# Building the matrices of each state-space block one block ahead, and the last two g_b tiles by seven products, in a gated two-branch encoder layer

## The chip, the core and the metric

The kernel runs on one core of one Trainium2 chip. The metric is device time in microseconds for one execution. The core has a matrix engine (PE in the profile, with its weight loads shown apart as PEld), two engines for elementwise work (DVE and ACT), a third one that here issues transfers and clears buffers (POOL), and SP, which issues weight loads. Each engine works through its own program in order: an instruction that waits holds up everything behind it on its engine. Engines wait for each other through semaphores.

## What is computed

One layer of a two-branch encoder on x of 512 positions by 2048 channels, in float32. Cut to what matters here:

```python
h = rmsnorm(x, norm_g)
v, bg, cg, za, u, zb, ga, gb = split(h @ w_in)          # 2048 wide each; u and zb 1024
ya = bg * causal_depthwise_conv(cg * v, conv_w)
ya = (ya * silu(za)) @ w_out_a
yb = gelu(s5_scan(u, a_re, a_im, log_dt, b_re, b_im, c_re, c_im, d_skip))
yb = yb * sigmoid(yb @ w_glu + b_glu)
yb = (yb * silu(zb)) @ w_out_b
m = sigmoid(ga) * ya + sigmoid(gb) * yb
return rmsnorm(x + m @ w_o, final_g)
```

`s5_scan` is a diagonal complex recurrence of 64 states for each of 64 groups of 16 channels, with an input matrix B, an output matrix C and a skip term.

## The kernel before

**Precision and tiles.** Activations and weights are split into a high part in the matrix engine's fp32r format and a low part (what is left). A product of two such numbers is taken as high·high + high·low + low·high, so a direct product of one 128x1024 weight tile with 512 positions takes 24 matrix instructions of 128x512 (lines 859 to 861). Such a tile is called a half gemm here, since two of them (16 x 128 input channels) make one output tile of 128 channels. Each weight tile is loaded from DRAM as `w_raw`, cast by ACT into `w_hi` (line 689), and DVE then takes `w_lo = w_raw - w_hi` (line 706). Two such pairs are made ahead of the half gemm that is being issued.

In what follows, half gemms and their weight tiles are numbered in the order of the casts: 0 to 17 make u, 18 to 49 the 16 tiles of g_b, 50 to 65 the 8 tiles of z_b, 66 to 73 the GLU, 74 to 89 the product with w_out_b. In names of the program, tile 27 is `w_hi_1321`, 28 is `w_hi_1366`, 29 is `w_hi_1400`, 30 is `w_hi_1451` and 31 is `w_hi_1508`.

**Seven products.** Later stages (c_g, v, z_a, b_g, most of g_a) take two output tiles at a time as a 2x2 block product with seven multiplications in place of eight (`seven`, lines 1101 and 1106). Each product uses 8 instructions of 128x512 and 8 of 128x256. The sums of weights that this needs are made partly by accumulating transfers on POOL and partly on DVE (lines 593 and 597).

**The stage of the state-space branch.** While PE works through the g_b and z_b tiles (`gate` and the loop over m behind it), a background generator `ssm_blocks` issues the recurrence in four blocks of 16 groups. After each half gemm `step(RATE)` lets it issue about RATE = 5.5 us of elementwise work; a scheduler then orders the instructions of each engine. For each block the generator calls:

- `front`: products of C and B with powers of the transition. DVE makes `F` (tiles `ssm_f`, 128x640) and, through `ssm_t`, the input matrices; ACT copies them to `ssm_bb` (line 358) and `ssm_sl` (line 375).
- `table`: ACT copies 16 columns of a base table (line 439) and a magnitude tile `g` (line 442), and DVE doubles the table at levels 4, 5 and 6 (18 small operations).
- `pe1`: 16 matrix instructions with `ssm_sl` (line 387), which give each chunk's input, and 16 with `ssm_bb` and `F` (line 395).
- `post`: ACT copies the chunk inputs to `h` (line 408, 8 instructions), makes `mi` (line 419, 8 instructions) and `el` from `F` (line 428, 4 instructions).
- `scan`: DVE multiplies by the table, runs two hardware scans (line 483), multiplies again, and leaves the states `x` and `h`.
- `skip`: ACT makes the skip term (line 519).
- `pe2` and `result`: PE forms the output from `mi`, `el` and the states (lines 507 and 510), DVE adds the skip term.

Before the change, the order for block i is: front(i), pe2(i-1), table levels 4 and 5, result(i-1), pe1(i), table level 6, post(i), loads for i+1, scan(i), skip(i).

The gate of a g_b tile (line 997) is an ACT instruction that waits until both half gemms of the tile are finished; its result goes to DRAM. After the last block, `gelu` and the GLU follow. The product with w_out_b multiplies each of its 16 output tiles by 1 + gate and stores it to `tb_d`.

Of the kernel before, what the change touches and what calls it, by code (L numbers as in the profile page):

```python
# [1 line left out]

# [1 line left out]

# [8 lines left out]
AF = mybir.ActivationFunctionType  # L13
ALU = mybir.AluOpType
ADD, SUB, MUL = ALU.add, ALU.subtract, ALU.mult
# [4 lines left out]
KD = D // P  # L20
# [6 lines left out]
SLOT = 1024  # L27
EPS = 1e-6
MAGIC = 12582912.0
RATE = 5.5  # L30
PRATE = 1.6
R7 = 1.2
WARM = 9
NR4 = 37
NA = 0
NAB = 2
NB7 = 14
LEAST = 0.6
NP7 = 4
OSTEP = 4.2  # L40
KORD = (0, 4, 1, 5, 2, 6, 3, 7)
HL = L // 2
EARLY = 2


# [490 lines left out]

def ssm_blocks(blocks):

    blocks[0].loads()
    yield 1  # L540
    for i, k in enumerate(blocks):
        yield from k.front()
        if i:
            blocks[i - 1].pe2()
            yield
        yield from k.table((4, 5))
        if i:
            yield from blocks[i - 1].result()
        k.pe1()
        yield from k.table((6,))  # L550
        yield from k.post()
        if i + 1 < len(blocks):
            blocks[i + 1].loads_u()
            blocks[i + 1].loads()
        yield from k.scan()
        yield from k.skip()
    yield 1
    blocks[-1].pe2()
    yield 1
    yield from blocks[-1].result()  # L560
# [162 lines left out]
def hybrid_kernel(ctx: ExitStack, tc: tile.TileContext, xT, x, cvec, fg, wu, wu7, wabc,  # L723
                  wgz, wgb, wga, wo, par, bs_d, be_d, ce_d, out):
    nc = tc.nc
    tt, ts, stt = _ew(nc)
    act = nc.scalar
# [11 lines left out]
    def psum():  # L739
        t = psp.tile([P, L], F32, tag="ps", name="ps")  # L740
        return t
# [3 lines left out]
    def wide(name, shape=(P, 2, L)):  # L745
        t = r4b.tile(list(shape), F32, tag="r4", name=name)
        return t

    def tmp():
        if r4b:  # L750
            return wide("tmp")[:, 0]
        t = tp_ctx.tile([P, L], F32, tag="tmp", name="tmp")
        return t
# [9 lines left out]
    W = WStream(c, 2, 2)  # L763
# [4 lines left out]
    for j in range(NA):  # L768
        for h in range(2):
            W.add(wga[j, h])  # L770
    for j in range(KD):
        for h in range(2):
            W.add(wgb[j, h])
    for m in range(8):
# [4 lines left out]
    for j in range(KD):  # L779
        W.add(wgb[j, 2])  # L780
    for j in range(NA, NAB):
        for h in range(2):
            W.add(wga[j, h])
    for j in range(0, KD, 2):
        for i in range(4):
            W.add7(wabc[j, i, 0], wabc[j + 1, i, 0], wabc[j + 1, i, 1], wabc[j, i, 1])
        i = NAB + j - 2
        if NAB <= i < NB7:
            W.add7(wga[i, 0], wga[i + 1, 0], wga[i + 1, 1], wga[i, 1])
    for j in range(NB7, KD):  # L790
        for h in range(2):
            W.add(wga[j, h])
# [31 lines left out]
    tb_d = [drp.tile([P, 2, L], F32, name=f"tb{j}") for j in range(KD // 2)]  # L824
# [4 lines left out]
    bg = []  # L829
# [127 lines left out]
    ps = psum()  # L957
# [42 lines left out]

    for j in range(NA):
        gate(ga_d[j // 2][:, j % 2], RATE)
    for j in range(KD):
        gate(gb_d[j], RATE)
    zb = []
    for m in range(8):
        ps = hgemm(RATE)
        if m % 2 == 0:
            zt = c.r4.tile([P, 2, L], F32, tag="r4", name="zb")
        tz = tmp()  # L1010
# [6 lines left out]
    for m in range(8):  # L1017
        ps = psum()
        gemm(ps, yg)
        th, g = tmp(), tmp()  # L1020
# [14 lines left out]
    def combine(k, out, yag=False):  # L1035
        y, t = wide("h_sum"), wide("h_t", (P, 4, HL))
        for i in range(2):
# [5 lines left out]
        if yag:  # L1043
            yield
        y11, y12, y21, y22 = y[:, 0, :HL], y[:, 0, HL:], y[:, 1, :HL], y[:, 1, HL:]
        if not yag:
# [7 lines left out]
        for i in range(2):  # L1054
            p = c.r4.tile([P, 2, 2, HL], F32R, tag="r4", name="h_comb")
            act.copy(p[:, :, 0], t[:, 2 * i:2 * i + 2])
# [6 lines left out]
    gq = []  # L1063

    def fetch_gb():
        if len(gq) < KD:
            t = tmp()
            nc.gpsimd.dma_start(t, gb_d[len(gq)])
            gq.append(t)
# [5 lines left out]
    for j in range(KD):  # L1075
        ps = psum()
        gemm(ps, yb, steps=1.15)
        th = gq[j]
        stt(th, th, 1.0, ps, ADD, MUL)
        nc.gpsimd.dma_start(tb_d[j // 2][:, j % 2], th)  # L1080
        fetch_gb()
    for j in range(NA, NAB):
        gate(ga_d[j // 2][:, j % 2], 4.2)
# [4 lines left out]
    def blocks(ops, sums):  # L1088
        y = [[ops[k0 + k][:, :, l0:l0 + HL] for k in range(8)] for k0, l0 in ((0, 0), (8, 0), (8, HL))]
        return y + [[sums[k][i] for k in range(8)] for i in range(4)]  # L1090

    def product(ps, acts, first, last, steps=R7):
# [10 lines left out]
        for k in range(8):  # L1103
            a = acts[k]
            flat = len(a.shape) == 2
            nc.tensor.matmul(ps[:, HL:], lo[:, k], a[:, :HL] if flat else a[:, 0], start=False,  # L1106
                             stop=last and k == 7, skip_group_check=True)
        step(steps)

    def seven(name, acts, steps=R7):  # L1110

        Y11, Y21, Y22, T1, T2, T3, T4 = acts
        o = wide(name)
        e1, pb = wide("half"), psum()
        product(pb, Y11, True, False, steps)
        act.copy(e1[:, 0], pb)
        e2, pd = wide("half"), psum()
        product(pd, T1, True, False, steps)
        act.copy(e2[:, 1], pd)
        product(pb, T2, False, False, steps)  # L1120
        act.copy(e1[:, 1], pb)
        product(pd, Y22, False, True, steps)
        tt(e1[:, 1], pd, e1[:, 1], ADD)
        product(pb, T3, False, False, steps)
        tt(e2[:, 1], pb, e2[:, 1], ADD)
        pa = psum()
        product(pa, Y21, True, True, steps)
        tt(e1[:, 0], pa, e1[:, 0], ADD)
        for i, e in enumerate((e1, e2)):
            if i:  # L1130
                product(pb, T4, False, True, steps)
                act.copy(e2[:, 0], pb)
            v = e.rearrange("p b (h l) -> p b h l", h=2)
            ov = o[:, i].rearrange("p (b l) -> p b l", b=2)
            if i:
                stt(ov, v[:, :, 0], -1.0, v[:, :, 1], MUL, SUB)
            else:
                tt(ov, v[:, :, 0], v[:, :, 1], ADD)
        return o
# [24 lines left out]
    def gate2(o, j):  # L1164
        t = wide("tz")
        act.activation(t, o, AF.Tanh, scale=0.5)
        nc.gpsimd.dma_start(ga_d[j // 2], t)
        yield

    hb = blocks(hp, th7)  # L1170
    for j in range(0, KD, 2):
        cc = seven("cg", hb)
        v = seven("v", hb)
        bg.append(conv(cc, v, j))
        z = seven("za", hb)
        bg.append(silu(cc, z))
        b = seven("bg", hb)
        bg.append(out_a(cc, b, j))
        i = NAB + j - 2
        if NAB <= i < NB7:  # L1180
            bg.append(gate2(seven("ga", hb), i))
    while bg:
        step()

# [17 lines left out]
    for _ in range(3):  # L1202
        step()
    for j in range(NB7, KD):
        gate(ga_d[j // 2][:, j % 2], 4.3)
# [14 lines left out]
    for j in range(NP7):  # L1220
        if j % 2 == 0:
            fetch_m()
        ps = psum()
        gemm(ps, yap[:8], last=False, steps=3.3)
        gemm(ps, yap[8:], first=False, steps=3.3)
        g, t = (v[:, j % 2] for v in mq[j // 2])
# [9 lines left out]
    def two(name):  # L1236
        t = c.r4.tile([P, 2, 2, HL], F32R, tag="r4", name=name)
        return t
# [64 lines left out]
    for j in range(NP7, KD, 2):  # L1303
# [3 lines left out]
        o = seven("wa", yb7, 1.7 if end else R7)  # L1307
# [129 lines left out]
    for i in range(2):  # L1437
        f = c.r4.tile([P, 1024], F32, tag="r4", name="fg")
# [23 lines left out]
    for t in range(2):  # L1462
        for a, b in [(0, L)] if t == 0 else [(0, HL), (HL, L)]:
            ps = psum()[:, :b - a]
# [85 lines left out]
```

## Time and profile before

| what | value |
|---|---|
| median of 3 runs | 1661.87 us |
| lowest and highest run | 1661.63 and 1663.71 us |
| profiled execution, its own time | 1661.74 us |
| span of that execution in the trace | 1659.9 us |
| DVE busy | 1301.0 us, 78% |
| ACT busy | 797.6 us, 48% |
| POOL busy | 238.3 us, 14% |

The span runs from the first to the last recorded instruction of the profiled execution; 1.8 us of that execution lie outside it. An engine's busy time is a mean over stages with different limits. The trace gives start and duration of each instruction, what an engine waited for ahead of it, and the clock that PE was granted.

### The profile page before, as it was taken

The numbers are of one execution on the slowest core, as the hardware profiler recorded it, in microseconds if no ns is written. First come the engines' busy times: TensorE is split into PE (matmuls) and PEld (weight loads), VectorE is DVE, ScalarE is ACT, GpSimd is POOL, SyncE is SP. The second block draws the span as 40 slices with busy tenths as digits, with TensorE's granted clock in tenths as the row PEclk, the third lists the DMA queues.
The fourth block names the chain that finished last, engine by engine and source line by source line (L and its number), as shares of the span: only waits on it lengthen the run. The fifth ranks groups of instructions, "written<-read, shape, count | busy, mean of one in ns | idle before, by whom it ended". The sixth has DMA issues, their size and how long they took to land.

```text
span 1659.9 us, 22983 instructions
## 1 busy us (share of the span) xinstructions
PE 1636.8 (99%) x8700; PEld 1397.8 (84%) x8700; DVE 1301.0 (78%) x1751; ACT 797.6 (48%) x1097; POOL 238.3 (14%) x387
## 2 busy tenths in 40 slices
PE   9999998899999999999999999999999999999997
PEld 7887887788888888888888888888888888888886
DVE  8996887895865687877878777777878787888497
ACT  6433556355522355555445555544545544446334
POOL 0012343211021101010100101001010231122000
PEclk9999999999999999999999999999999999999999
DMA  8333563543364677777776777777776788997783
GB/s 312 117 102 87 146 177 115 133 140 77 134 215 134 165 186 205 186 205 206 206 203 178 207 192 201 201 202 215 184 210 180 290 272 239 268 320 252 234 329 102
DMA packets 93199, 320.62 MB, mean 193 GB/s; under 512 B 12672, under 2 KB 12928, under 8 KB 93088
## 3 DMA queue, kind: packets, MB, share of 16 engines
q1 hardware_dynamic: 58752, 204.65, 35.8%
q0 software_dynamic: 33616, 113.40, 29.7%
q8 instruction: 68, 1.11, 0.3%
q10 hardware_dynamic: 720, 1.10, 0.2%
q14 instruction: 43, 0.35, 0.1%
HBM read 287.51 MB, written 25.30 MB: 188 GB/s over the span
## 4 chain that ended last, share of the span: by engine, by line
PE 94%; ACT 2%; DVE 2%; issue 1%; DMA 0%; DVEq 0%; SPq 0%; ACTq 0%
PE ps L1101 34%; PE ps L1106 18%; PE ps L1324 10%; PE ps L859 9%; PE ps L860 9%; PE ps L861 9%; PE ps L944 2%; PE ps L942 2%; PE ps L943 2%; PE ps L387 1%; PE ps L395 1%; ACT w_hi L689 1%; DVE ssm_t L66 0%; DVE w_lo L706 0%; PE ps L510 0%
## 5 line engine op out<-in xcount | busy, mean ns | idle before, releaser
L689 ACT CAST w_hi<-w_raw 128x1024 fp32r<-128x1024 f32 (+2 forms) x459 | 478.7, 1045 | 662.0 <-PE ps L1101 281.1
L706 DVE TENSOR_TENSOR w_lo<-w_raw,w_hi 128x1024 fp32r<-128x1024 f32 (+2 forms) x459 | 556.5, 1214 | 193.1 <-ACT w_hi L689 189.6
L1101 PE MATMUL ps<-h_comb,w_hi 128*128 128x512 f32 x1408 | 352.5, 392 | 0.0
L1101 PEld LDWEIGHTS ps<-h_comb,w_hi 128*128 128x128 f32 x1408 | 253.2, 189 | 45.2
L861 PE MATMUL ps<-pair,w_lo 128*128 128x512 f32 x720 | 280.7, 390 | 3.3 <-DVE w_lo L706 3.3
L859 PE MATMUL ps<-pair,w_hi 128*128 128x512 f32 x720 | 280.8, 391 | 3.2 <-ACT w_hi L689 2.7
L860 PE MATMUL ps<-pair,w_hi 128*128 128x512 f32 x720 | 280.4, 390 | 0.4 <-DVE pair L66 0.4
L1101 PE MATMUL ps<-pair,w_hi 128*128 128x512 f32 x1056 | 264.4, 392 | 0.0
L1101 PEld LDWEIGHTS ps<-pair,w_hi 128*128 128x128 f32 x1056 | 190.1, 189 | 34.1
L1106 PEld LDWEIGHTS ps<-h_comb,w_lo 128*128 128x128 f32 x1408 | 192.1, 190 | 13.7
L1106 PE MATMUL ps<-h_comb,w_lo 128*128 128x256 f32 x1408 | 196.3, 282 | 0.0
L859 PEld LDWEIGHTS ps<-pair,w_hi 128*128 128x128 f32 x720 | 135.0, 188 | 33.3 <-ACT w_hi L689 3.3
L861 PEld LDWEIGHTS ps<-pair,w_lo 128*128 128x128 f32 x720 | 135.1, 188 | 32.6 <-DVE w_lo L706 4.4
L860 PEld LDWEIGHTS ps<-pair,w_hi 128*128 128x128 f32 x720 | 135.2, 188 | 28.9 <-DVE pair L66 1.0
L1106 PEld LDWEIGHTS ps<-pair,w_lo 128*128 128x128 f32 x1056 | 144.1, 190 | 10.3
L1106 PE MATMUL ps<-pair,w_lo 128*128 128x256 f32 x1056 | 147.2, 282 | 0.0
L66 DVE TENSOR_TENSOR half<-ps,half 128x512 f32<-128x512 f32 x132 | 90.6, 686 | 66.5 <-PE ps L1106 66.5
L673 POOL DMA_DIRECT2D w_raw<-in_wabc_dram x64 | 55.2, 862 | 555.4 <-DMA w_raw<-in_wabc_dram 379.0
L1324 PE MATMUL ps<-w_hi,pair 128*128 128x512 f32 x192 | 60.8, 389 | 0.0
L597 DVE TENSOR_TENSOR w_raw<-w_raw 128x1024 f32<-128x1024 f32 x44 | 53.9, 1225 | 1.5
L593 DVE TENSOR_TENSOR w_raw<-w_raw 128x1024 f32<-128x1024 f32 x44 | 53.9, 1224 | 1.5
L1324 PE MATMUL ps<-w_hi,m_half 128*128 128x512 f32 x160 | 50.8, 389 | 0.0
(218 smaller groups left out, 1750.9 us busy)
## 6 DMA issues: line engine op xcount, KB each, us to landing
w_raw<-in_wabc_dram SPq DMA_DIRECT2D x160, 512.0 KB, 4.3
w_raw<-in_wga_dram SPq DMA_DIRECT2D x76, 512.0 KB, 5.1
w_raw<-in_wabc_dram POOLq DMA_DIRECT2D x64, 512.0 KB, 6.3
w_raw<-in_wo_dram SPq DMA_DIRECT2D x52, 512.0 KB, 6.1
w_raw<-in_wgb_dram SPq DMA_DIRECT2D x48, 512.0 KB, 3.8
w_raw<-in_wgz_dram SPq DMA_DIRECT2D x24, 512.0 KB, 3.4
w_raw<-in_wga_dram POOLq DMA_DIRECT2D x24, 512.0 KB, 7.1
m_r<-m POOLq DMA_DIRECT2D x32, 256.0 KB, 5.7
```

Of the source, the lines that this page charges most:

```text
L66: return v.tensor_tensor(out=o, in0=a, in1=b, op=op)
L593: tt(out=b11["x"], in0=b11["x"], in1=s1["x"], op=ADD)
L597: tt(out=s1["x"], in0=b12["x"], in1=b11["x"], op=ADD)
L673: nc.gpsimd.dma_start(box["x"], src.rearrange("p a b -> p (a b)"), accum_op=ADD)
L689: nc.scalar.copy(hi[:, a:b], raw[:, a:b])
L706: nc.vector.tensor_tensor(out=lo[:, a:b], in0=raw[:, a:b], in1=hi.bitcast(F32)[:, a:b], op=SUB)
L859: nc.tensor.matmul(ps, hi[:, k], a[:, 0], start=first and k == 0, stop=False)
L860: nc.tensor.matmul(ps, hi[:, k], a[:, 1], start=False, stop=False)
L861: nc.tensor.matmul(ps, lo[:, k], a[:, 0], start=False, stop=last and k == 7)
L1101: nc.tensor.matmul(ps if flat else both, hi[:, k], a, start=first and k == 0, stop=False, skip_group_check=True)
L1106: nc.tensor.matmul(ps[:, HL:], lo[:, k], a[:, :HL] if flat else a[:, 0], start=False, stop=last and k == 7, skip_group_check=True)
L1324: nc.tensor.matmul(ps, l, r[:, k2, c0:c1], start=first and k2 == i == 0, stop=last and k2 == 1 and i == 2, skip_group_check=True)
```

## The change

The generator now makes the matrices of block i+1 between the chunk inputs of block i and its scan. `front(0)` stands ahead of the loop. Inside, the loads for the next block come first, then the table (levels 4 and 5, pe2 of the block in front, level 6, its result), `pe1(i)`, four steps of `front(i+1)`, the first two steps of `post(i)` (the copies to `h`), the rest of `front(i+1)`, the rest of `post(i)`, and the scan. RATE goes from 5.5 to 6.1.

The last two of the 16 g_b tiles leave the direct stage (`NGB = 14`). They are made in one call of `seven`, after the first round of c_g, v, z_a and b_g. Until then the two w_out_b tiles that belong to them go to `tb_d[7]` as they are; a new background step, `gate_b`, reads them back, takes tanh of the two g_b tiles on ACT, multiplies on DVE and writes them again. In the numbering above, z_b now follows at 46, the GLU at 62 and w_out_b at 70.

```diff
-RATE = 5.5
+RATE = 6.1
+NGB = 14
+GB7 = {0: 14}
...
 def ssm_blocks(blocks):
     blocks[0].loads()
     yield 1
+    yield from blocks[0].front()
     for i, k in enumerate(blocks):
-        yield from k.front()
+        last = i + 1 == len(blocks)
+        if not last:
+            blocks[i + 1].loads_u()
+            blocks[i + 1].loads()
+        yield from k.table((4, 5))
         if i:
             blocks[i - 1].pe2()
             yield
-        yield from k.table((4, 5))
+        if not last:
+            yield from k.table((6,))
         if i:
             yield from blocks[i - 1].result()
         k.pe1()
-        yield from k.table((6,))
-        yield from k.post()
-        if i + 1 < len(blocks):
-            blocks[i + 1].loads_u()
-            blocks[i + 1].loads()
+        f = k.table((6,)) if last else blocks[i + 1].front()
+        for _ in islice(f, 4):
+            yield
+        p = k.post()
+        for _ in islice(p, 2):
+            yield
+        yield from f
+        yield from p
         yield from k.scan()
         yield from k.skip()
...
-    for j in range(KD):
+    for j in range(NGB):
         for h in range(2):
             W.add(wgb[j, h])
...
             W.add7(wga[i, 0], wga[i + 1, 0], wga[i + 1, 1], wga[i, 1])
+        if j in GB7:
+            i = GB7[j]
+            W.add7(wgb[i, 0], wgb[i + 1, 0], wgb[i + 1, 1], wgb[i, 1])
...
-        th = gq[j]
-        stt(th, th, 1.0, ps, ADD, MUL)
+        if j < NGB:
+            th = gq[j]
+            stt(th, th, 1.0, ps, ADD, MUL)
+        else:
+            th = tmp()
+            act.copy(th, ps)
         nc.gpsimd.dma_start(tb_d[j // 2][:, j % 2], th)
...
+    def gate_b(o, j):
+        t, r = wide("tz"), wide("tb_w")
+        nc.gpsimd.dma_start(r, tb_d[j // 2])
+        act.activation(t, o, AF.Tanh, scale=0.5)
+        yield
+        stt(r, t, 1.0, r, ADD, MUL)
+        nc.gpsimd.dma_start(tb_d[j // 2], r)
+        yield
...
+        if j in GB7:
+            bg.append(gate_b(seven("gb", hb), GB7[j]))
```

In the changed kernel the lines shift: 859 to 861 become 876 to 878, 387 becomes 391, 395 becomes 399, 689 becomes 703, 706 becomes 720, 997 becomes 1014, 358 and 375 become 362 and 379, 408, 419 and 428 become 412, 423 and 432, 439 and 442 become 443 and 446.

**First place: PE, the first matrix instructions of block 0.** These are the last rows of a half gemm and the start of `pe1(0)`, before the change. `w_hi_1400` is tile 29.

```order
L859 MATMUL ps_1505<-pair_870,w_hi_1400 128x512
L860 MATMUL ps_1505<-pair_870,w_hi_1400 128x512
L861 MATMUL ps_1505<-pair_870,w_lo_1453 128x512
L387 MATMUL ps_1544<-ssm_ug_947,ssm_sl_1479 128x128
L387 MATMUL ps_1545<-ssm_ug_947,ssm_sl_1479 128x128
```

The same place in the changed kernel, where `w_hi_1336` is tile 27:

```order
L876 MATMUL ps_1422<-pair_870,w_hi_1336 128x512
L877 MATMUL ps_1422<-pair_870,w_hi_1336 128x512
L878 MATMUL ps_1422<-pair_870,w_lo_1368 128x512
L391 MATMUL ps_1544<-ssm_ug_947,ssm_sl_1415 128x128
L391 MATMUL ps_1545<-ssm_ug_947,ssm_sl_1415 128x128
```

`pe1(0)` has moved from behind half gemm 29 to behind half gemm 27.

**Second place: ACT, at the same point.** Before the change; line 997 is the gate, `tmp_1502` that of half gemms 26 and 27, `tmp_1673` that of 28 and 29.

```order
L689 CAST w_hi_1400<-w_raw_1319 128x1024
L997 ACTIVATE tmp_1394<-ps_1318 128x512
L997 ACTIVATE tmp_1502<-ps_1397 128x512
L689 CAST w_hi_1451<-w_raw_1364 128x1024
L689 CAST w_hi_1508<-w_raw_1398 128x1024
L358 COPY ssm_bb_1437<-ssm_ft_1428 64x8x16 x4
L375 COPY ssm_sl_1479<-ssm_t_1480 64x8x64 x2
L439 COPY ssm_rr_1490<-ssm_base_1244 128x8x16
L439 COPY ssm_ri_1491<-ssm_base_1244 128x8x16
L442 COPY ssm_g_1495<-ssm_keep_304 128x1024
L689 CAST w_hi_1587<-w_raw_1449 128x1024
L375 COPY ssm_sl_1479<-ssm_t_1480 64x8x64 x2
```

In the changed kernel `tmp_1585` is the gate of 26 and 27, `tmp_1697` that of 28 and 29, and `w_hi_1425`, `w_hi_1508` and `w_hi_1591` are tiles 29, 30 and 31.

```order
L1014 ACTIVATE tmp_1585<-ps_1422 128x512
L703 CAST w_hi_1425<-w_raw_1334 128x1024
L703 CAST w_hi_1508<-w_raw_1364 128x1024
L379 COPY ssm_sl_1415<-ssm_t_1416 64x8x64 x2
L362 COPY ssm_bb_1403<-ssm_ft_1394 64x8x16 x4
L703 CAST w_hi_1591<-w_raw_1423 128x1024
L379 COPY ssm_sl_1415<-ssm_t_1416 64x8x64 x2
L1014 ACTIVATE tmp_1697<-ps_1588 128x512
L443 COPY ssm_rr_1488<-ssm_base_1244 128x8x16
L443 COPY ssm_ri_1489<-ssm_base_1244 128x8x16
L446 COPY ssm_g_1493<-ssm_keep_304 128x1024
L703 CAST w_hi_1648<-w_raw_1506 128x1024
```

The cast of tile 29 now stands behind the gate of half gemms 26 and 27 instead of ahead of it, and the start of the table stands behind the gate of 28 and 29 instead of ahead of it.

**Third place: ACT, ahead of the scan of block 0.** Before the change; `tmp_1745` is the gate of half gemms 30 and 31, `w_hi_1679` and `w_hi_1713` are tiles 33 and 34.

```order
L408 COPY ssm_h_1622<-ps_1555 64x512
L428 COPY ssm_el_1637<-ssm_f_1429 64x512
L419 ACTIVATE ssm_mi_1627<-ps_1564,cvec_t_75 32x8x64 x2
L419 ACTIVATE ssm_mi_1627<-ps_1564,cvec_t_75 32x8x48 x2
L419 ACTIVATE ssm_mi_1627<-ps_1564,cvec_t_75 32x8x32 x2
L419 ACTIVATE ssm_mi_1627<-ps_1564,cvec_t_75 32x8x16 x2
L428 COPY ssm_el_1637<-ssm_f_1433 64x512
L428 COPY ssm_el_1637<-ssm_f_1429 64x512
L428 COPY ssm_el_1637<-ssm_f_1433 64x512
L689 CAST w_hi_1679<-w_raw_1506 128x1024
L689 CAST w_hi_1713<-w_raw_1585 128x1024
L997 ACTIVATE tmp_1745<-ps_1676 128x512
```

In the changed kernel `w_hi_1745` is tile 34, `tmp_1899` the gate of half gemms 32 and 33, and `ssm_sl_1676` belongs to block 1.

```order
L703 CAST w_hi_1745<-w_raw_1646 128x1024
L379 COPY ssm_sl_1676<-ssm_t_1677 64x8x64 x2
L1014 ACTIVATE tmp_1899<-ps_1778 128x512
L379 COPY ssm_sl_1676<-ssm_t_1677 64x8x64 x2
L423 ACTIVATE ssm_mi_1687<-ps_1564,cvec_t_75 32x8x64 x2
L423 ACTIVATE ssm_mi_1687<-ps_1564,cvec_t_75 32x8x48 x2
L423 ACTIVATE ssm_mi_1687<-ps_1564,cvec_t_75 32x8x32 x2
L423 ACTIVATE ssm_mi_1687<-ps_1564,cvec_t_75 32x8x16 x2
L432 COPY ssm_el_1731<-ssm_f_1395 64x512
L432 COPY ssm_el_1731<-ssm_f_1399 64x512
L432 COPY ssm_el_1731<-ssm_f_1395 64x512
L432 COPY ssm_el_1731<-ssm_f_1399 64x512
```

The copies to `mi` and `el` of block 0 stood ahead of the gate of half gemms 30 and 31; they now stand behind the gate of 32 and 33. The scan's second product takes a buffer that the third of these `el` copies (the last reader of `ssm_f_1395`) sets free.

More of the change, by code (lines that the diff above doesn't have):

```diff
@@ L1 @@
 from contextlib import ExitStack
+from itertools import islice
 import numpy as np
@@ L1002, in hybrid_kernel @@
         gate(ga_d[j // 2][:, j % 2], RATE)
-    for j in range(KD):
+    for j in range(NGB):
         gate(gb_d[j], RATE)
@@ L1065, in fetch_gb @@
     def fetch_gb():
-        if len(gq) < KD:
+        if len(gq) < NGB:
             t = tmp()
```

## The prediction

> **What bounds the kernel now.** I read the page first, then PE's waits, then the stretches of the stage in which the change works, then the chain and the timelines there.
>
> ```profile
> span 1659.9 us, 22983 instructions
> PE 1636.8 (99%) x8700; PEld 1397.8 (84%) x8700; DVE 1301.0 (78%) x1751; ACT 797.6 (48%) x1097; POOL 238.3 (14%) x387
> PE 94%; ACT 2%; DVE 2%; issue 1%; DMA 0%; DVEq 0%; SPq 0%; ACTq 0%
> PE ps L387 <- ACT ssm_sl L375: 6.3, 3, 3.0
> PE ps L861 <- DVE w_lo L706: 3.3, 3, 1.4
> PE ps L859 <- ACT w_hi L689: 2.7, 2, 1.6
> ```
>
> PE is busy 99% of the span and is 94% of the chain. The last three rows say for whom PE waited: total, times, longest. There is little idle time to win: 12.3 us in these rows, and they lie in the state-space stage.
>
> ```profile
> 162.00:184.00 22.00, 20.78 (x129) 17.94 (x130) 16.91 (x26) 15.72 (x27) 15.06 (x26) 0.92 0.69 164
> 250.00:272.00 22.00, 17.30 (x122) 13.40 (x120) 16.82 (x28) 12.52 (x25) 1.19 (x3) 1.00 0.30 99
> 316.00:338.00 22.00, 19.01 (x154) 16.01 (x153) 19.97 (x39) 13.68 (x29) 3.88 (x8) 0.92 0.35 104
> sum 352.00, PE 339.52 PEld 279.62 DVE 282.45 ACT 169.54 POOL 82.61; mean PE 21.22 PEld 17.48 DVE 17.65 ACT 10.60 POOL 5.16
> ```
>
> Each row is a stretch: busy time of PE, PEld, DVE, ACT, POOL, then the granted clock. The sum, over 96 to 448 us, leaves PE 12.5 us idle. In that stretch DVE is 80% busy, so PE runs there with a second engine close behind. PE is held in three places, and the clock mean of 0.92 in two of the stretches is 8% of 22 us, 1.76 us lost in each: the price of half speed for twice that, 3.5 us. So a wait here costs its own length and something over 1.7 us behind it.
>
> The Trainium skill, page "TensorE: Matmul & The Clock Gate", section "Why this matters for your kernels", wants no idle gap over about 3 us between bursts of matmuls, since the clock gate then goes back to half. By that rule, which speaks against this change, each long wait costs its length plus a slow window; without it the sum below would be some 6 us less. The two 0.92 rows agree, and go further: there a longest wait of 3.0 us was enough.
>
> **What the seven products save.** The group of direct instructions in the stage, then starts of pieces on the chain:
>
> ```profile
> L859 PE MATMUL ps<-pair,w_hi 128*128 128x512 f32 x400 | 156.4, 392 | 3.2 <-ACT w_hi L689 2.7 <-ACT pair L760 0.5
> 1020.31 1.84 PE ps L1101 x8
> ...
> 1023.10 1.84 PE ps L1101 x8
> ...
> 420.10 0.23 PE ps L860
> ```
>
> The busy time of one instruction (392 ns) is no price, since neighbours overlap: the chain shows a direct one starting every 0.23 us, and a product, eight instructions of each kind, every 1023.10 - 1020.31 = 2.79 us and seven of them 19.5. A half gemm has 24 instructions: 24 x 0.227 = 5.44 us. Two g_b tiles are four half gemms, 21.8 us. The change removes 21.8 and adds 19.5: **-2.2 us** of PE work. ACT and DVE have three more weight tiles to split, beside seven more products; in the later stages no PE wait is in the list above, so I cost these, the two output tiles by copy, and the second pass over `tb_d[7]` at 0. What covers them is the background work's slack. If that cover is gone, the price is one 1.05 us tanh, one 1.22 us product and two transfers, bounded by their landing times in these rows:
>
> ```profile
> L1152 ACT ACTIVATE tz<-za 128x1024 f32<-128x1024 f32 x8 | 8.4, 1054 | 0.0
> L76 DVE SCALAR_TENSOR_TENSOR za<-tz,za 128x1024 f32<-128x1024 f32 x8 | 9.8, 1220 | 0.0
> tb_r<-tb POOLq DMA_DIRECT2D x8, 512.0 KB, 6.1
> ```
>
> So 0 to +14.5 us (1.1 + 1.2 + 6.1 + 6.1); below nothing it can't go, as all of it is added. I take 0, as the similar steps on z_a show 0.0 idle ahead.
>
> **The first seam: block 0's matrices (+8.6).** Rows of ACT, then one of DVE, then the chain:
>
> ```profile
> 150.10 0.60 ACT L997 ACTIVATE tmp<-ps 128x512 f32<-128x512 f32 x1 [9.56 <-PE ps L861]
> 150.59 1.99 ACT L689 CAST w_hi<-w_raw 128x1024 fp32r<-128x1024 f32 x2
> 157.73 1.23 ACT L358 COPY ssm_bb<-ssm_ft 64x128 f32<-64x128 f32 x4 [5.15 <-DVE ssm_ft L66]
> 158.98 1.25 ACT L375 COPY ssm_sl<-ssm_t 64x512 f32<-64x512 f32 x2
> 160.26 0.30 ACT L439 COPY ssm_rr<-ssm_base 128x128 f32<-128x128 f32 x1
> 160.67 1.04 ACT L442 COPY ssm_g<-ssm_keep 128x1024 f32<-128x1024 f32 x1
> 162.56 1.25 ACT L375 COPY ssm_sl<-ssm_t 64x512 f32<-64x512 f32 x2
> 151.66 1.23 DVE L706 TENSOR_TENSOR w_lo<-w_raw,w_hi 128x1024 fp32r<-128x1024 f32 x1 [7.42 <-ACT w_hi L689]
> 163.22 3.49 PE ps L387 x31
> 169.40 0.43 PE ps L859
> ```
>
> The gate at 150.10 is that of half gemms 26 and 27; ACT stood behind it for 9.56 us, and the casts and everything of `front(0)` behind them on DVE start only then. The path from there to the last `ssm_sl` (163.8) is covered by half gemms 28 and 29, which run to 161, so PE idles 2.3 us, then does `pe1(0)` at half clock (163.22 to 169.40, 6.2 us) and goes on.
>
> In the changed order `pe1(0)` stands right behind half gemm 27, and the cast of tile 29 has gone behind that same gate. DVE's second half of `front(0)` still begins at 151.66, with the subtraction for tile 29 in the place of tile 30's, and the path holds as many casts and subtractions as before. It loses the three copies of the table (160.26 to 161.6, 1.35 us), and the four to `bb` (1.23) now stand behind the first pair of `sl` instead of ahead: 163.8 - 2.6 = **161.1** for the last `sl`. PE has finished 27 at 150.1 and has nothing else in order: idle 11.0 us. `pe1(0)` takes 6.0, mostly at half clock, and half gemms 28 and 29 end at 161.1 + 6.0 + 10.9 = 178.0. The same work was done at 169.40 before: **+8.6**.
>
> **The second seam: table, `el` and scan of block 0 (+19.4).**
>
> ```profile
> 160.88 0.28 DVE L66 TENSOR_TENSOR ssm_rr<-ssm_rr,ssm_keep 128x128 f32<-128x128 f32 x1
> 167.71 0.68 DVE L66 TENSOR_TENSOR ssm_ri<-ssm_ri,ssm_t 128x512 f32<-128x512 f32 x1
> 170.20 3.75 ACT L419 ACTIVATE ssm_mi<-ps,cvec_t 32x512 f32<-32x512 f32 x8
> 173.96 1.88 ACT L428 COPY ssm_el<-ssm_f 64x512 f32<-64x512 f32 x3
> 179.23 1.22 DVE L66 TENSOR_TENSOR ssm_t<-ssm_h,ssm_ri 128x1024 f32<-128x1024 f32 x1
> 195.42 1.23 DVE L706 TENSOR_TENSOR w_lo<-w_raw,w_hi 128x1024 fp32r<-128x1024 f32 x1
> 196.56 2.46 DVE L66 TENSOR_TENSOR ssm_h<-ssm_h,ssm_t 64x1024 f32<-64x1024 f32 x2
> 212.02 2.19 PE ps L387 x31
> 216.11 0.43 PE ps L859
> ```
>
> The table now starts behind the gate of 28 and 29, so at 178.5 instead of 160.3; the table (18 operations between the first two rows, 7.5 us with another one of 0.6 among them) and the first four of `front(1)` hold the low parts of tiles 32 and 33: I count 2.5 us of PE idle. Half gemm 33 ends at 178.0 + 4 x 5.44 + 2.5 = 202.3. Behind its gate ACT does two `sl` copies (1.2), the eight of `mi` (3.75) and three of `el` (1.9), to 210.3 with its handovers; then the buffer for the second scan product is free. From that product to the subtraction that stands behind the scan were 195.42 - 179.23 = 16.2 us, so tile 35's low part is ready at 210.3 + 16.2 + 1.2 = 227.7, and the states at 230.2. PE finishes half gemm 34 at 207.7, does `pe1(1)` (216.11 - 212.02 = 4.1), four instructions of `pe2(0)` and two of half gemm 35 until 214.7 at the latest, and then stands before tile 35's low part: **13.0 us idle**, 1.4 more at the states, and a slow window. Half gemm 36 starts at 238.6 and 37 at 244.1. Before, the same work was done at 216.11: a lag of 28.0, **19.4** more than at the first seam.
>
> **The blocks behind (+32.5), and the end.**
>
> ```profile
> 276.14 0.43 PE ps L860
> 337.23 0.43 PE ps L859
> ```
>
> Block 1 repeats the pattern: its table start stands behind the gate of half gemms 36 and 37 (250), tile 39's low part behind that table (261.2, where PE is ready at 254.9: 5.5 idle, 1.3 slow), `mi` and `el` behind 39's gate, the scan from 281.9 to 300.6, and tile 42's low part behind it. Half gemm 43 starts at 307.5 and 46 at 323.8. Before, `pe1(2)` was over at 276.14 and half gemm 46 began 14 instructions (3.2 us) later, at 279.3: lag 44.5, +16.5. Block 2 again: table behind the gate of 45 (324.5), 5.9 us idle and 1.3 slow for tile 47, scan from 351.8, states at 370.5 with PE idle for 11.2, half gemm 54 at 399.1 against 338.6 (337.23 and six instructions more): lag 60.5, +16.0. Behind the last block nothing is moved; of before's own waits there some 1 us of 1.4 goes.
>
> The full sum is 8.6 + 19.4 + 32.5 - 1.0 - 2.2 = +57.3, or 1661.74 + 57.3 = 1719 us. What I trust least in it is the wait for `el`: where the buffers come free earlier than I read, seams two to four cost only the tables' gates and a scan that partly fits beside two half gemms. The nearest measured bound for a scan that PE waits for is the old stretch from 250 to 272 with 4.7 us idle; with 8 for each (4.7, the slow window of 1.7, and about 1.5 for the table) the sum is 8.6 + 3 x 8 - 3.2 = +29.4, or 1691 us. I lean to the full walk, as its waits stand in the program's order, and go a quarter of the way to the other end: **1712 us**. The profiled execution (1661.74) is within 0.2 us of the median of the runs, 1661.87, so the sum is made against both alike.
>
> **Rivals.**
>
> (a) It does what it says: matrices ready early, so the 6.3 us for `ssm_sl` go, with the two slow windows (3.5 us), and the seven products save 2.2: 1661.7 - 12.0 = 1650 us. For it: that wait is PE's longest, and blocks 1 to 3 do get their matrices a block earlier. Against it: block 0's do not, and the scan's late end replaces them. Chance 0.08.
>
> (b) Only the first seam is lost and the rest is caught up, because DVE has 20% of slack: 8.6 - 2.2, less up to 4 us for `ssm_sl` in blocks 2 and 3: +2.4 to +6.4, or 1664 to 1668 us, slower than before though little. It decides if tables and `el` of blocks 1 to 3 turn out to be on time. Against it: DVE can't use slack while it stands behind ACT, and ACT stands behind gates of half gemms just done. Chance 0.10; about half of that is within 0.2%.
>
> (c) The later stage, not the scan, decides: the second pass over `tb_d[7]` holds a buffer and PE waits for it, up to 14.5 us on top of the lighter walk (1691): 1706. Chance 0.06; it lies inside the range.
>
> (d) The walk as it stands, with a lighter and a full end, 1691 to 1719: chance 0.76.
>
> **How the numbers follow.** The range has to hold 0.8: it takes (c) and (d), 0.82 together, with room on both sides. Below 1691 I allow 17 us, as the 8 us for each of three seams may be 2.3, the smallest wait that the old order shows at such a place; above 1719 a further 16, the 14.5 us of (c) and one slow window. That is **1674 to 1735 us**. Left out are (a) and (b), 0.18. About 0.2%, 3.3 us, is what a measurement of this kernel can tell from no change. Faster by more than that: (a), 0.08. Within it: the low half of (b), 0.05. Slower: the rest, 0.87.
>
> **What would show each step.** In the profile of the changed kernel: PE idle about 11 us just behind 150, released by `ssm_sl`; `pe1(0)` starting near 161 where it started at 163.2; the table's copies behind the gate near 178; the first scan's second product near 210, with the third `el` copy as its releaser; waits of PE for `w_lo` of 5 to 13 us in the g_b stage, and more 0.9 clocks; seven products in the place of four half gemms with no wait by them. If PE stays busy for 96% of the stretch from 96 to 448 us, I am wrong. If the wait near 150 is there and the later ones are not, it is (b); then my error is the scan's start, not the order.

## The result, and the profile after

The changed kernel takes **1726.26 us** (median of 4 runs, 1725.56 to 1726.78) where the kernel before took 1661.84 us in the same session: 1.0385 times as long, 95% interval 1.0367 to 1.0403, or some 64 us. The profiled execution has a span of 1724.4 us, 64.5 more than before.

The page of the changed kernel: the span, busy time of the engines, the granted clock in 40 slices, and the chain by engine.

```profile
span 1724.4 us, 23012 instructions
PE 1649.0 (96%) x8716; PEld 1407.5 (82%) x8716; DVE 1310.4 (76%) x1760; ACT 805.1 (47%) x1105; POOL 238.9 (14%) x387
PEclk9998988889999999999999999999999999999999
PE 88%; DVE 6%; ACT 3%; issue 2%; DMA 0%; POOL 0%; SPq 0%; DVEq 0%; ACTq 0%; POOLq 0%
```

PE is idle for 1724.4 - 1649.0 = 75.4 us, against 1659.9 - 1636.8 = 23.1 before: 52.3 us more. It is also busy for 12.2 us more, though the seven products take work away: that is work at a lower clock. Together these are the 64.5. Both lie early: below 9 tenths the clock is only in slices 4 and 6 to 9, counted from 0, so between 129 and 388 us.

The same stretch of the state-space stage, 96 to 448 us, in one row: length, busy time of PE, PEld, DVE, ACT, POOL with instructions, then the granted clock, the DMA share and GB/s.

```profile
96.00:448.00 352.00, 288.10 (x1546) 236.84 (x1546) 241.79 (x415) 136.37 (x231) 81.43 (x148) 0.91 0.41 106
```

PE idles for 63.9 us there (12.5 before), which holds nearly all of the 52.3. DVE and ACT are less busy too, 242 and 136 us where they were 282 and 170. So no engine became the bound; each waits for another. The top rows of three lists of the changed kernel say for whom, between 140 and 460 us: engine, line, waited for, total, times, longest.

```profile
PE ps L878 <- DVE w_lo L720: 33.0, 7, 12.0
PE ps L514 <- DVE ssm_h L70: 10.9, 1, 10.9
PE ps L391 <- ACT ssm_sl L379: 10.9, 1, 10.9
PE ps L511 <- issue: 5.6, 3, 2.9
```
```profile
DVE ssm_rr L70 <- ACT ssm_rr L443: 47.9, 3, 17.8
DVE w_lo L720 <- ACT w_hi L703: 33.0, 8, 12.5
DVE ssm_t L70 <- ACT ssm_el L432: 14.0, 2, 7.0
```
```profile
ACT tmp L1014 <- PE ps L878: 74.1, 7, 16.7
...
ACT w_hi L703 <- DMA w_raw<-in_wgb_dram: 15.6, 6, 4.9
...
ACT w_hi L703 <- DMA w_raw<-in_wgz_dram: 4.8, 3, 3.7
```

Read together they close a ring. PE waits 33.0 us for low parts that DVE makes; DVE waits 47.9 us, in three pieces, for the start of a table that ACT copies; ACT waits 74.1 us, in seven pieces, at the gate (line 1014) until PE has finished a half gemm. The last two ACT rows are weight tiles that were not there in time, 20.4 us; no such row stood in ACT's list before. The gates' wait did stand there:

```profile
ACT tmp L997 <- PE ps L861: 51.9, 6, 10.3
```

So what is new is less this wait than what stands behind it: DVE's list before had no row for the table or for `el`.

One turn of the ring, from the timelines of ACT, DVE and PE (start, duration, engine, instruction, idle time before it and its releaser):

```profile
178.18 0.60 ACT L1014 ACTIVATE tmp<-ps 128x512 f32<-128x512 f32 x1 [16.68 <-PE ps L878]
178.80 0.30 ACT L443 COPY ssm_rr<-ssm_base 128x128 f32<-128x128 f32 x1
...
201.14 1.05 ACT L703 CAST w_hi<-w_raw 128x1024 fp32r<-128x1024 f32 x1 [3.47 <-DMA w_raw<-in_wgb_dram]
...
204.76 0.60 ACT L1014 ACTIVATE tmp<-ps 128x512 f32<-128x512 f32 x1
...
207.50 3.75 ACT L423 ACTIVATE ssm_mi<-ps,cvec_t 32x512 f32<-32x512 f32 x8
211.27 2.52 ACT L432 COPY ssm_el<-ssm_f 64x512 f32<-64x512 f32 x4
```
```profile
179.13 0.29 DVE L70 TENSOR_TENSOR ssm_rr<-ssm_rr,ssm_keep 128x128 f32<-128x128 f32 x1 [17.78 <-ACT ssm_rr L443]
...
213.18 1.23 DVE L70 TENSOR_TENSOR ssm_t<-ssm_h,ssm_ri 128x1024 f32<-128x1024 f32 x1 [6.99 <-ACT ssm_el L432]
...
229.38 1.23 DVE L720 TENSOR_TENSOR w_lo<-w_raw,w_hi 128x1024 fp32r<-128x1024 f32 x1
```
```profile
160.91 4.21 PE L391 MATMUL ps<-ssm_ug,ssm_sl 64*128 64x128 f32 x32 [10.89 <-ACT ssm_sl L379]
...
230.66 0.79 PE L878 MATMUL ps<-pair,w_lo 128*128 128x512 f32 x1 [12.00 <-DVE w_lo L720]
```

PE started 10.89 us late at 160.91; so the gate came at 178.18; so the table, which needs nothing of PE, came at 178.80 and DVE stood 17.78 us for it. The gate of half gemms 32 and 33, the next but one, came at 204.76, with `mi` and `el` behind it; DVE stood 6.99 us for a buffer that the copies to `el` still read, did the scan, and only then the low part at 229.38, for which PE stood 12.00 us. That delays the gates behind it, and block 1 begins the same way.

The cast at 201.14 is the one late weight tile that lies on this path. The chain shows that it was issued late and was not slow: the load starts right behind the copies to `bb` and takes 3.42 us, where the median of such loads is 3.7.

```profile
197.38 0.30 ACT ssm_bb L362
...
197.70 3.42 DMA w_raw<-in_wgb_dram
```

### The profile page after: what moved, and what is told of

It is laid out like the page before. It is cut to its first block, busy times and chain, and to the rows that moved or that the text cites. A ratio compares the mean times of both kernels' runs of the same rounds, so it can differ in the third digit from the quotient of the medians.

```text
span 1724.4 us, 23012 instructions
## 1 busy us (share of the span) xinstructions
PE 1649.0 (96%) x8716; PEld 1407.5 (82%) x8716; DVE 1310.4 (76%) x1760; ACT 805.1 (47%) x1105; POOL 238.9 (14%) x387
## 4 chain that ended last, share of the span: by engine, by line
PE 88%; DVE 6%; ACT 3%; issue 2%; DMA 0%; POOL 0%; SPq 0%; DVEq 0%; ACTq 0%; POOLq 0%
PE ps L1122 34%; PE ps L1127 17%; PE ps L1356 9%; PE ps L878 8%; PE ps L876 8%; PE ps L877 8%; DVE ssm_t L70 2%; PE ps L961 1%; PE ps L960 1%; PE ps L959 1%; DVE ssm_h L70 1%; DVE ssm_h L487 1%; DVE w_lo L720 1%; ACT ssm_mi L423 0%; ACT ssm_sl L379 0%
## 5 line engine op out<-in xcount | busy, mean ns | idle before, releaser
L1122 PE MATMUL ps<-h_comb,w_hi 128*128 128x512 f32 x1440 | 360.6, 392 | 0.0
L878 PE MATMUL ps<-pair,w_lo 128*128 128x512 f32 x688 | 272.4, 396 | 33.7 <-DVE w_lo L720 33.7
L1122 PEld LDWEIGHTS ps<-h_comb,w_hi 128*128 128x128 f32 x1440 | 259.0, 189 | 46.3
L876 PE MATMUL ps<-pair,w_hi 128*128 128x512 f32 x688 | 271.8, 396 | 3.9 <-ACT w_hi L703 3.2
L877 PE MATMUL ps<-pair,w_hi 128*128 128x512 f32 x688 | 271.2, 394 | 0.2 <-DVE pair L70 0.2
L1122 PE MATMUL ps<-pair,w_hi 128*128 128x512 f32 x1080 | 270.4, 392 | 0.0
L1127 PEld LDWEIGHTS ps<-h_comb,w_lo 128*128 128x128 f32 x1440 | 196.5, 190 | 14.0
L1127 PE MATMUL ps<-h_comb,w_lo 128*128 128x256 f32 x1440 | 200.8, 282 | 0.0
L1127 PEld LDWEIGHTS ps<-pair,w_lo 128*128 128x128 f32 x1080 | 147.3, 190 | 10.5
L687 POOL DMA_DIRECT2D w_raw<-in_wabc_dram x64 | 55.3, 864 | 538.9 <-DMA w_raw<-in_wabc_dram 372.2
```

The costliest lines, as they stand in the source:

```text
L687: nc.gpsimd.dma_start(box["x"], src.rearrange("p a b -> p (a b)"), accum_op=ADD)
L876: nc.tensor.matmul(ps, hi[:, k], a[:, 0], start=first and k == 0, stop=False)
L877: nc.tensor.matmul(ps, hi[:, k], a[:, 1], start=False, stop=False)
L878: nc.tensor.matmul(ps, lo[:, k], a[:, 0], start=False, stop=last and k == 7)
L1122: nc.tensor.matmul(ps if flat else both, hi[:, k], a, start=first and k == 0, stop=False, skip_group_check=True)
```

## The experiments

Ratios are to the kernel before, run in the same session, with 95% intervals; a ratio is turned into microseconds by 1662 us. The difference of two ratios is uncertain by about 0.002, some 3.5 us.

| kernel | RATE | blocks | ratio | us |
|---|---|---|---|---|
| e2, before with RATE alone | 6.1 | old | 1.0045 [1.0032, 1.0059] | +7.5 |
| e1, seven products alone | 5.5 | old | 1.0055 [1.0041, 1.0068] | +9.1 |
| e7, both | 6.1 | old | 1.0037 [1.0023, 1.0051] | +6.1 |
| the change | 6.1 | new | 1.0385 [1.0367, 1.0403] | +64.0 |
| e3, the change | 5.5 | new | 1.0380 [1.0366, 1.0394] | +63.2 |
| e4, loads late | 6.1 | new | 1.0380 [1.0366, 1.0395] | +63.2 |
| e5, product in `sl` | 6.1 | new | 1.0382 [1.0368, 1.0396] | +63.5 |
| e6, e5 and post first | 6.1 | new | 1.0333 [1.0318, 1.0347] | +55.3 |
| e9, no gate wait | 6.1 | new | 1.0101 [1.0085, 1.0118] | +16.8 |
| e10, e7 with no gate wait | 6.1 | old | 0.9954 [0.9937, 0.9971] | -7.6 |
| e11, e6 with no gate wait | 6.1 | new | 1.0025 [1.0014, 1.0036] | +4.2 |
| e8, e7 with a rest | 6.3 | old | 1.0013 [1.0004, 1.0022] | +2.2 |
| e12, e7 with a gate moved | 6.1 | old | 0.9999 [0.9989, 1.0010] | -0.2 |

### The parts of the change: e1, e2, e7, e3

**e1** keeps the old blocks and RATE, and makes the last two g_b tiles by seven products.

```diff
 RATE = 5.5
+NGB = 14
+GB7 = {0: 14}
...
```

> The generator and RATE of before, with only the two g_b tiles by seven products. By my theory (the seven products save 2.2 us and everything beside them is hidden) 1659.6 us, 1658 to 1661, with the waits of the state-space stage as before. Rival (the second pass over tb_d[7], the three further weight tiles or the longer POOL queue make PE wait): 1662 to 1676, with a wait of PE near the first rounds of seven products.

**e2** is the kernel before with the new RATE and nothing else.

```diff
-RATE = 5.5
+RATE = 6.1
```

> The kernel before with RATE 6.1 and nothing else. In the program's order pe1 of block 0 then stands behind half gemm 27 as in the change, but the table, mi and el of block 0 stay ahead of the gates. By my theory only the first seam is lost: PE idle about 11 to 12 us near 150 and about 1671 us (1667 to 1676). Rival (the first wait too comes from the early matrices and their loads): no wait there beyond 3 us and about 1662 us.

**e7** is e1 with the new RATE: the whole change but for the order of the blocks.

```diff
 GB7 = {0: 14}
-RATE = 5.5
+RATE = 6.1
```

> The change without its generator: the blocks' order of before, RATE 6.1, the two g_b tiles by seven products. If the 12.3 us wait for the gelu's tiles in e1 is the cover of four half gemms that left the stage, and RATE 6.1 makes up for it, the wait is gone here and the time is that of e2 less 2.2: 1668.6 us (1667 to 1671), and the new order of the blocks alone costs 57 us of the change. Rival (the seven products cost some 9 us wherever they stand): 1680 us.

PE's longest wait between 140 and 460 us, first in e1, then in e2:

```profile
PE ps L866 <- ACT pair L764: 13.2, 4, 12.3
```
```profile
PE ps L387 <- ACT ssm_sl L375: 16.7, 3, 10.6
```

In e1 PE has no wait at the seven products. Its new wait of 12.3 us is at the GLU, which needs the gelu of the last block: four half gemms fewer, at 5.5 us of background work each, leave 22 us of that work without a place ahead of it. The time fell into the range of the rival, by a wait that neither side had named. In e2 the background runs ahead instead, `pe1(0)` is issued early and PE stands 10.6 us for `ssm_sl`: the first seam of the prediction, with no new order at all. With both (e7) the GLU wait is gone and the first seam stays. The products themselves are then worth 6.1 - 7.5 = -1.4 us, which fits the -2.2 of the prediction and, at 3.5 us of uncertainty, nothing as well.

So the new order of the blocks costs 64.0 - 6.1 = **57.9 us**, nine tenths of the loss (at the old RATE, e3 less e1, 54.1).

**e3** is the whole change with the old RATE.

```diff
-RATE = 6.1
+RATE = 5.5
```

> The whole change with RATE back at 5.5. pe1 of block 0 then stands behind half gemm 29 again; tables still stand behind the gate of the tile in front, mi and el too. By my theory the first wait falls back to 2 to 3 us, the others stay in part: about 1698 us (1685 to 1710). Rival (RATE is the cause of all of it): 1660 us.

PE's main waits in e3:

```profile
PE ps L878 <- DVE w_lo L720: 35.7, 7, 12.6
PE ps L876 <- ACT pair L774: 13.8, 3, 13.0
PE ps L876 <- ACT w_hi L703: 10.3, 3, 3.9
PE ps L391 <- ACT ssm_sl L379: 1.4, 1, 1.4
```

The first seam shrinks from 10.9 to 1.4 us, and the GLU's wait of 13.0 us is back; the ring of 35.7 us stays. Both sides missed this run: neither had the GLU's wait in it, nor the 10.3 us for casts, 3.2 in the change.

### Waits taken out inside the ring: e4, e5, e6

**e4** issues the loads for the next block behind the table, not ahead of it.

```diff
-        if not last:
-            blocks[i + 1].loads_u()
-            blocks[i + 1].loads()
         yield from k.table((4, 5))
...
+        if not last:
+            blocks[i + 1].loads_u()
+            blocks[i + 1].loads()
         k.pe1()
```

> The change, with the loads for the next block issued behind the table instead of ahead of it. In the program's order the table's copies then stand ahead of the gates, while mi and el stay behind them. By my theory the first wait stays (11 to 13 us), the waits of PE behind tables (2.5, 5.6 and 6.0 us with their slow clock) go, and those behind the scans stay: about 1708 us (1702 to 1714). Rival (the early loads take buffers, and this is the whole loss): below 1675 us. Rival (mi and el alone decide): 1724 us, as now.

**e5** gives the scan's second product a buffer that is long free, so that it need not wait for `el`.

```diff
-        t1 = self.new([P, QB, NCH], "t1")
+        t1 = self.sl.rearrange("p q r s -> p q (r s)")
```

> The change, with the scan's second product written into the tile of the input matrices, which is dead by then, instead of a new buffer: it no longer has to wait for the third copy of el. By my theory this buffer is what holds the scans of blocks 0 and 1 (DVE idle 7.0 us each for el in the change): the scan starts some 8 us earlier, PE's waits behind the scans shrink from 12, 6.9 and 10.9 us to about 5 each, and the time falls to about 1706 us (1698 to 1714). Rival (the scan starts late because the next block's matrices stand ahead of it on DVE and ACT, and the buffer only names the last of several waits): 1720 to 1727 us, the same waits under other names.

**e6** is e5 with `mi` and `el` ahead of the next block's matrices.

```diff
-        p = k.post()
-        for _ in islice(p, 2):
-            yield
+        yield from k.post()
         yield from f
-        yield from p
```

> As e5, and the copies of mi and el issued ahead of the next block's matrices, which then stand between el and the scan. By my theory (mi and el late) a little below e5: 1700 us (1690 to 1710). Rival (matrices ahead of the scan, wherever mi and el stand): within 3 us of e5.

DVE's main waits in e4 (longest only), in e5, then the longest in e6:

```profile
DVE ssm_t L70 <- ACT ssm_h L412: 44.9, 3, 18.3
```
```profile
DVE ssm_rr L70 <- ACT ssm_rr L443: 55.6, 3, 19.0
...
DVE ssm_x L70 <- ACT ssm_el L432: 10.5, 3, 4.2
```
```profile
DVE ssm_rr L70 <- ACT ssm_rr L443: 55.6, 3, 19.1
```

In e4 the 47.9 us for the table are gone but for 0.4, and 44.9 us for the copies to `h` have come: these stand behind a gate too, in block 0 behind the one of half gemms 30 and 31. In e5 the 14.0 us at `ssm_t` are gone, and the wait for the table has grown by 7.7 us, with 10.5 us for `el` at a later place. Neither changed the time beyond the uncertainty. For e5 that is what its rival gave: the buffer only names the last of several waits. e4's time is the one that its rival gave, but e5 takes away the wait on which that rival rests, and there the time stays too. e6, between its two forecasts, gained about 8 us, and DVE still waits 55.6 us for the table. Once the ring is closed, a wait that is named in it says where it shows, not what it would give back.

### The ring cut at the gate: e9, e10, e11

In **e9** the 14 direct g_b gates read a tile that is ready long before, with the same shape and the same place in ACT's order. So e9, e10 and e11 leave the gates out of what they compute, and only their times are of use.

```diff
-        act.activation(th, ps, AF.Tanh, scale=0.5)
+        act.activation(th, hp[0][:, 0].bitcast(F32) if steps == RATE else ps, AF.Tanh, scale=0.5)
```

> The whole change, with the tanh of each of the 14 g_b tiles reading a tile of h that has long been in place instead of its sums: the gates are left out of the result, their instruction stays. They then run early, and every other instruction of PE, DVE and ACT keeps its place in the order of the change. By my theory (ACT, and POOL behind it, stand behind the gate of the half gemm that is running, and DVE's table and scan with them: 47.9 us of DVE's idle time in the change) the waits for sl, w_lo and the states go almost entirely: 1650 to 1672 us. Rival (the next block's matrices ahead of the scan lengthen DVE's own chain, whatever ACT does): 1690 us or more.

**e10** has the same edit in e7, so with the old blocks.

```diff
-        act.activation(th, ps, AF.Tanh, scale=0.5)
+        act.activation(th, hp[0][:, 0].bitcast(F32) if steps == RATE else ps, AF.Tanh, scale=0.5)
```

> e7 (blocks' order of before, RATE 6.1, seven products) with the gates left out of the result in the same way. By my theory its first wait (10.6 us with a slow clock) goes too, since it stands behind the gate of half gemms 26 and 27: 1652 to 1658 us. With e9 it tells what the new order costs where no gate stands in the way: near 0 by my theory, 20 us or more by the rival.

**e11** has it in e6.

```diff
-        act.activation(th, ps, AF.Tanh, scale=0.5)
+        act.activation(th, hp[0][:, 0].bitcast(F32) if steps == RATE else ps, AF.Tanh, scale=0.5)
```

> e6 (second product of the scan in a dead tile, mi and el ahead of the next block's matrices) with the gates left out of the result as in e9. What the new order costs without gates is 24.6 us (1680.5 against 1655.9 in e10), and DVE there still waits 14.0 us for el, ACT 29.1 us for late weight tiles. If el and the buffer behind it are most of it: 1658 to 1667 us. If the late weight tiles (buffers held by the early matrices) or the matrices' place ahead of the scan are: 1672 us or more.

Rows of DVE's waits in e9, of ACT's in e9, then of ACT's in e11:

```profile
DVE w_lo L720 <- ACT w_hi L703: 28.5, 13, 5.8
DVE ssm_t L70 <- ACT ssm_el L432: 14.0, 2, 7.0
```
```profile
ACT w_hi L703 <- DMA w_raw<-in_wgb_dram: 29.1, 6, 9.5
```
```profile
ACT w_hi L700 <- DMA w_raw<-in_wgb_dram: 10.2, 3, 5.2
```

e9 came out between its two forecasts, e10 and e11 within theirs. DVE's 47.9 us for the table are gone from e9's list but for 0.5. The new order still costs something: e9 stands 16.8 + 7.6 = 24.4 us above e10, where the theory of the gates alone had near 0 and its rival, the next block's matrices ahead of the scan, 20 or more. So the gates are not the whole cause. With their wait the order cost 57.9. So **33.5 us** (some 5 either way) of the order's cost exist only while ACT stands behind the gates. Of the other 24.4, e11 leaves 4.2 + 7.6 = 11.8: about 12.6 us belong to what e11 has and e9 has not, the free buffer and the early `mi` and `el`; in it the late weight tiles fall from 29.1 to 10.2 us. The remaining 11.8 were not taken apart; the matrices' place ahead of the scan, which e11 keeps, is a candidate that was not tried by itself. The edit has a second effect that was not separated: a PSUM buffer that no gate reads comes free earlier. It is in e9 and e10 alike, so the difference of the two holds only what the orders make of it.

### Can the first seam be avoided: e8, e12

**e8** lets the background rest for one half gemm ahead of `pe1(0)`, at a RATE of 6.3.

```diff
-RATE = 6.1
+RATE = 6.3
...
+        if not i:
+            yield 1
         k.pe1()
```

> e7 with RATE 6.3, and the generator resting for one half gemm ahead of pe1 of block 0, so that it stands behind half gemm 29 as before. By my theory the first seam's 10.6 us of e2 shrink to 2.3 and the time is 1668.6 - 9 = 1659.6 us (1656 to 1664), a little below the kernel before. Rival (other waits take its place, since all else comes half a block later against the GLU): 1664 to 1672 us.

**e12** leaves e7's order and puts the gate of half gemms 26 and 27 behind the cast of tile 31, by a bias of zero that is made from that cast's result.

```diff
+    hold_gate = {4: 31}
...
-        act.activation(th, ps, AF.Tanh, scale=0.5)
+        if j in hold_gate:
+            while W.na <= hold_gate[j]:
+                W._hi()
+            z = c.cst.tile([P, 1], F32, name="gate_z")
+            act.activation(z, W.hl[hold_gate[j]][1].bitcast(F32)[:, 0:1], AF.Copy, scale=0.0)
+            act.activation(th, ps, AF.Tanh, scale=0.5, bias=z)
+        else:
+            act.activation(th, ps, AF.Tanh, scale=0.5)
```

> e7 with one gate moved: the tanh of half gemms 26 and 27 takes a bias of zeros made from weight tile 31, so that on ACT it stands behind the casts of tiles 29 to 31 and the copies to sl, and not ahead of them. Nothing else moves. By my theory of the first seam the 10.6 us wait falls to about 3.5 (what e10 has left there, the loads of the matrices), and the time to 1660.5 us (1659 to 1663), level with the kernel before. Rival (that wait comes from DVE's work for front(0), not from the gate): 1667 us or more.

PE's longest waits in e8, then in e12:

```profile
PE ps L870 <- DVE w_lo L712: 8.5, 4, 2.8
PE ps L391 <- ACT ssm_sl L379: 3.9, 2, 3.5
```
```profile
PE ps L391 <- ACT ssm_sl L379: 10.1, 3, 4.9
```

e8 loses the long first wait and gets 8.5 us of short ones for low parts, as its rival had it. e12 cuts the longest wait for `ssm_sl` from 10.6 us to 4.9 by getting one gate out of ACT's way, and is level with the kernel before. No version that computes the whole layer was faster than the kernel before.

## Why the prediction held, and what was mis-sized

The forecast was slower, 1712 us, with a full walk of 1719; 1726.3 lies inside the range. By its steps:

- **First seam.** The walk had PE idle for 11.0 us and `pe1(0)` from 161.1; the trace shows 10.89 us and 160.91. e2 and e7 add what the walk did not separate: this seam comes from RATE, not from the order of the blocks, and RATE alone costs 7.5 us (8.6 in the walk).
- **Second seam.** Table behind the gate at 178.5 (measured 178.80), low part of tile 35 after 13.0 us of idle PE (12.00). The scan's second product was released as foreseen by the third `el` copy; it was set at 210.3 and came at 213.18: the gate at 204.76 was to be at 202.3, and a cast ahead of it waited 3.47 us for its weight tile.
- **Blocks 1 and 2.** PE's waits of 5.5 us at tile 39, 5.9 at tile 47 and 11.2 at block 2's states were foreseen (5.57, 6.02 and 10.94). Rows of PE for the last two and for other waits there, then of ACT:

```profile
287.46 0.66 PE L876 MATMUL ps<-pair,w_hi 128*128 128x512 f32 x1 [2.95 <-ACT w_hi L703]
...
339.56 0.80 PE L878 MATMUL ps<-pair,w_lo 128*128 128x512 f32 x1 [6.02 <-DVE w_lo L720]
361.48 0.86 PE L511 MATMUL ps<-ssm_u,ssm_mi 128*64 128x128 f32 x8 [2.86 <-issue]
376.58 0.47 PE L514 MATMUL ps<-ssm_h,ssm_el 128*64 128x127 f32 x1 [10.94 <-DVE ssm_h L70]
```
```profile
283.83 2.51 ACT L432 COPY ssm_el<-ssm_f 64x512 f32<-64x512 f32 x4
286.37 1.04 ACT L703 CAST w_hi<-w_raw 128x1024 fp32r<-128x1024 f32 x1
...
347.75 0.60 ACT L1028 ACTIVATE tmp<-ps 128x512 f32<-128x512 f32 x1 [2.52 <-PE ps L878]
348.24 1.21 ACT L362 COPY ssm_bb<-ssm_ft 64x128 f32<-64x128 f32 x4
...
357.88 3.75 ACT L423 ACTIVATE ssm_mi<-ps,cvec_t 32x512 f32<-32x512 f32 x8
```

- **What the walk lacked**, some 7 us (1726 against 1719), can be followed in starts. At block 0's gate the trace is 2.5 us behind the walk, from the weight tile that came late; the walk took every one as loaded in time. At block 1's second product it is 3.8 behind (285.73 against 281.9), at block 2's table 3.7 (328.18 against 324.5), and at block 2's scan 6.1 (357.89 against 351.8): there the copies to `bb` stood behind the tanh of a z_b tile at 347.75, and DVE 3.64 us behind these copies. The other late weight tiles came while DVE was at its scans, so the 20.4 us are no term of the sum. The wait of 2.95 us is none for a weight tile either: its cast starts at 286.37, as soon as ACT is through with `el`. The 2.86 us that have no releaser end at 361.48, as the copies to `mi` which that instruction reads come to their end (357.88 + 3.75 = 361.63). All this is read from the trace, not tried by itself.
- **The step that was wrong** is the last one: going a quarter of the way to a lighter end of 1691, because buffers might come free earlier than read. e5 made that buffer free at once and the time stayed at +63.5 us. The doubt was about one wait, while the ring has another one behind it; the discount of 7 us had no ground. The lighter end also added waits up as terms, 8 us for each seam, where the full walk followed the order around the ring. e4 and e5 show that they aren't terms: taking out 47.9 us of one of DVE's waits, or 14.0 of another, was worth 0 within the uncertainty.
- **Seven products.** -2.2 us in the sum, with 0 for all that hangs on them; -1.4 measured, some 3.5 us either way. The cover that the prediction named for the 0, the slack of the background work, is real and is made by RATE: at 5.5 it is gone and the GLU waits 12.3 us (e1), within the 0 to 14.5 that were priced, though not by the transfers that the prediction put there.
- **Slow clock.** The walk priced 1.3 to 1.8 us behind a long wait, and said that 3.0 us was enough for it; in one of its two rows the only wait is shorter, 2.28 us. PE was busy for 12.2 us more, net of what the products save, so this term is a fifth of the loss and was right to be kept.

Of the rivals, (a), that it does what it says, failed at the point named against it: the scan's late end took the place of the waits for `ssm_sl`. (b), the loss is caught up by DVE's slack, failed for the reason given, DVE stands behind ACT and ACT behind gates; e9 and e10 show this for 33.5 of the 57.9 us. (c) did not appear: PE has no wait by `tb_d[7]`.

## What to carry to other kernels

When one engine in order both drains the matrix engine's results and feeds the work that the matrix engine will wait for, look at which feeding instructions stand behind a drain; moving them there can close a ring, in which a wait of the matrix engine comes back at each turn, here in each of the first three blocks. In such a ring don't add up the waits of the profile, and don't expect one that is taken out to be given back (two here gave nothing): cut it at the drain, which here held some 33 of 58 us, or keep the feeding work ahead of it. A number that sets the pace of background work (RATE) belongs to the amount of foreground work that it is spread over, so price it together with a change of that amount.

## What was not expected of the hardware

The clock. Windows of the changed kernel:

```profile
184.00:206.00 22.00, 19.48 (x84) 15.12 (x83) 17.35 (x26) 10.17 (x18) 1.43 (x3) 1.00 0.10 37
...
272.00:294.00 22.00, 18.29 (x124) 14.89 (x122) 13.36 (x12) 13.87 (x25) 2.53 (x4) 0.92 0.26 88
...
316.00:338.00 22.00, 17.54 (x78) 14.20 (x76) 9.50 (x22) 3.48 (x6) 5.80 (x12) 1.00 0.35 64
338.00:360.00 22.00, 19.06 (x70) 15.04 (x70) 14.98 (x21) 14.14 (x25) 2.56 (x4) 0.84 0.13 47
```

Before the change, PE's start of `pe1(0)`, in the row from 162 to 184 us that the prediction shows with 0.92:

```profile
163.22 3.49 PE L387 MATMUL ps<-ssm_ug,ssm_sl 64*128 64x128 f32 x32 [2.28 <-ACT ssm_sl L375]
```

From 184 to 206 us PE idles for 2.5 us in three waits, the longest 1.47, and the clock stays at 1.00. From 272 to 294 us a wait of 2.95 us (row at 287.46), with one of 0.41 ahead of it, goes with 0.92, and the first matrix instruction behind it takes 0.66 us, where the mean of that form was 392 ns before the change. Before the change a single wait of 2.28 us goes with 0.92. The Trainium skill, page "TensorE: Matmul & The Clock Gate", section "Why this matters for your kernels", puts the limit at gaps over about 3 us; in these rows it lies lower, as 1.47 us left the clock alone and 2.28 did not. And a row's clock is not that of its waits: the wait of 6.02 us that ended at 339.56 began in a row that shows 1.00, and the slow work is in the next one, 0.84.
